# The ends of two routed mixture-of-experts stages in another order, with eight modulation products moved to a later stage

## The chip, the cores and the metric

One core of one Trainium2 chip runs the whole program. The metric is the device time of one execution in microseconds (us). The core's engines are TensorE (PE in the profile; PEld is its weight load), VectorE (DVE), ScalarE (ACT), GpSimd (POOL) and SyncE (SP), which issues the transfers.

## The reference

The program computes two blocks over 256 tokens of 1024 numbers in float32. The first has two layers. Each mixes tokens (attention of two kinds), normalizes, and then runs a routed mixture of 16 experts, two per token:

```python
def first_block(x, ...):
    for l in range(DEPTH):            # 2
        mix = even_mixer(...) if l % 2 == 0 else odd_mixer(...)
        x = layer_norm(ALPHA * x + mix, ln_g[l, 0], ln_b[l, 0])
        ffn = routed_moe(x, router_w, router_b, moe_w_gate[l], moe_w_up[l], moe_w_down[l])
        x = layer_norm(ALPHA * x + ffn, ln_g[l, 1], ln_b[l, 1])
    return x

# in routed_moe, for each expert e:
    h = jax.nn.silu(xt @ w_gate[e]) * (xt @ w_up[e])
    y = y + gates[:, e:e + 1] * (h @ w_down[e])
```

The second block has six sublayers (four swiglu feed-forwards, one hybrid recurrence, one mLSTM). In each, the input is normalized by its root mean square and shifted and scaled by a modulation vector, the product of a condition vector with a large matrix ("ada").

## The kernel before

There are ten stages, A to J, run in this order. A is the even attention (0 to about 131 us in the profile), B the routed experts of layer 0 (to about 361), C the odd attention (to about 475), D the routed experts of layer 1 (to about 709), E, G, H and J the feed-forwards, F the hybrid, I the mLSTM.

**Weights.** Nearly all time goes to matrix products with weights that are used once. SyncE streams them as transfers of 1 MB, two chunks of 128x1024 float32 each, into a ring of blocks (`load_weights`, L521); a transfer needs a free block, and a block is free when both of its chunks are used up. Most products are made of two halves of the weight: ScalarE copies a chunk to the shorter type fp32r (L598) and VectorE makes the difference to the original, again in fp32r (L599). TensorE multiplies with both (`mm`, L607). The expert stages use the chunks as they are and split the features instead. `SPLIT_AHEAD` gives the splits of a stage a priority by which the scheduler places them ahead of their use.

**Ada.** The modulation vectors don't use TensorE: VectorE multiplies a chunk with the broadcast condition vector and sums over the row (`ada_step`, L560). `ADA` says how many of the 144 chunks each stage takes, as running ends (A the first 15, C the next 10, E the next 35). A plan spreads them evenly over the stage's own chunks.

**Routed stages.** The 16 experts go in pairs 0 to 7. For each pair, `gate_up` makes two PSUM banks on TensorE; `hidden` runs silu on ScalarE (L1377) and a product on VectorE (L1378); `turn` transposes the result on TensorE (L612) and copies it out (L1386); `down` multiplies with the second weights and takes each half of the result out of PSUM twice, the high part by ScalarE (L1406) and the low part by VectorE (L1407); `combine` multiplies both with the gates and adds the result to x (L1426). Each pair's `turn`, `combine` and `down` run behind the next pair's `gate_up`. Behind `gate_up` of pair 5 all engines load a count and branch on it (`overflow`, L1441 and L1442): the branch's body deals with experts that got too many tokens, and isn't entered in these runs.

**The end of a routed stage.** For pairs 6 and 7, `combine` adds into four PSUM banks, one for each token half (t) and column half (n), which start with the product of the identity and x. `first_splits` makes the first splits of the next stage's weights here (three in B, four in D), and the evacuations of pair 7 are placed behind these (`first`). Then `normed` takes statistics of each bank (L816), their mean and variance (L821), the root (L822) and the affine part (L833 to L838), first for token half 0, then 1. The next stage starts on each token half: in C with transposes (L612), a copy (L1613) and a difference (L1614); in E with sums of squares (L874), a reciprocal root (L876 to L880), a scaling (L916), transposes and features (L683 to L691).

**Order.** Within `behind(...)` an instruction is placed after the named ones; `pinned()` places what is in it behind the last TensorE instruction. `spin` is a row of transposes of a constant whose result isn't used (`SPIN` has their counts: entry 3 stands between D and E, entry 4 between B and C).

Of the kernel before, what the change touches and what calls it, by code (L numbers as in the profile page):

```python
# [9 lines left out]
F32 = mybir.dt.float32  # L10
# [4 lines left out]
OP = mybir.AluOpType  # L15
# [40 lines left out]
ADA = {'A': 15, 'C': 25, 'E': 60, 'F': 64, 'G': 96, 'H': 132, 'I': 140, 'J': 144}  # L56
# [342 lines left out]
SPIN = 20, 12, 8, 50, 20  # L399
# [8 lines left out]
class Net:  # L408
    NBLK = 23

    def __init__(self, ctx, tc, aps, phases, plan=None, at=None):
        self.tc, self.nc, self.aps, self.phases = tc, tc.nc, aps, phases
        self.blk = ctx.enter_context(tc.tile_pool(name="blk", bufs=1))
        self.cst = ctx.enter_context(tc.tile_pool(name="cst", bufs=1))
        self.sm = ctx.enter_context(tc.tile_pool(name="sm", bufs=2))
        self.pp = ctx.enter_context(tc.tile_pool(name="pp", bufs=4, space=bass.MemoryType.PSUM))
        self.issue_at, self.at = plan, at or {}
        self.free = [(-64, 0, b) for b in range(self.NBLK if plan is not None else 64)]
        self.own, self.nfree = {}, 0
# [9 lines left out]
        self.pre, self.guard, self.guarded, self.ada_held, self.evac = [], [], 0, 0, None  # L429
        self.first, self.last, self.left = {}, {}, {}  # L430
# [368 lines left out]
    def normed(self, x, get, tok, gb=None):  # L799
# [9 lines left out]
        def fin(t, n, o):  # L809
# [5 lines left out]
            with self.behind(*first[:n]):  # L815
                v.bn_stats(st[:, t, n, :], o)  # L816
# [49 lines left out]
    def rstd(self, t):  # L866
# [8 lines left out]
        if n_ == 2:  # L875
            nc.vector.tensor_tensor(r, ss[:, 0:1], ss[:, 1:2], op=OP.add)  # L876
        else:
            nc.vector.tensor_reduce(r, ss[:, :n_], axis=AX.X, op=OP.add)
# [370 lines left out]
    def phase_moe(self, l):  # L1249
# [131 lines left out]
        def turn(h, hT):  # L1381
# [4 lines left out]
            nc.scalar.activation(hT, pt, AF.Copy)  # L1386
            return hT

        def down(pr, hT, gsl, nextw, then, first=()):
# [13 lines left out]
            def leave(n):  # L1403
                ns = PIECES[0][n]
                with self.behind(*first):
                    self.evac = nc.scalar.activation(yy[:, 0, ns], y[n], AF.Copy, scale=gsl[:, pr % 2, :])  # L1406
                    v.scalar_tensor_tensor(yy[:, 1, ns], y[n], gsl[:, pr % 2, :], yy[:, 0, ns].bitcast(F32),  # L1407
                                           op0=OP.mult, op1=OP.subtract)
                then(n, yy)

            for n in range(2):
                some(((n, 0), (n, 1)))
                some(((n, 2), (n, 3)))
                leave(n)
            return uy, yy

        def combine(pr, yy, PT, n, c=None):

            ns = PIECES[0][n]
            for t in range(2):  # L1420
                o = c[t, n] if c else self.ph()
                for j in range(2):
                    self.mm(o, PT[pr % 2][:, t * 128:(t + 1) * 128], yy[:, j, ns], j == 0 and not c,
# [109 lines left out]
        for s in range(8):  # L1533
# [36 lines left out]
        with pinned():  # L1570
            h = hs.pop(7)
            hT = turn(h, self.w2([128, 4, 128]))
            c = {}
            for t in range(2):
# [847 lines left out]
```

## Time and profile before

| | us |
|---|---|
| median of 3 runs (lowest to highest) | 1877.28 (1875.49 to 1878.21) |
| the profiled execution's own time | 1873.63 |
| its span | 1871.7 |
| TensorE busy | 1824.0 (97%) |
| VectorE busy | 1229.0 (66%) |
| ScalarE busy | 929.4 (50%) |
| mean of the transfers | 271 GB/s |

The share of an engine is a mean over stages with different limits. In a timeline row the first number is the time from the span's start, the second the duration of the group, "x8" the number of instructions in it, and the bracket the idle time of that engine before it and what ended it. TensorE's products of float32 (identity, `down`) appear as two records each, so that eight records are four products of the program; those of fp32r (`combine`) appear as one. PEclk is the granted clock as a share of full speed.

### The profile page before, as it was taken

What the parts mean: (1) busy time and instruction counts of PE and PEld (TensorE: products, weight loads), DVE (VectorE), ACT (ScalarE), POOL (GpSimd) and SP (SyncE); (2) the same over time, 40 slices, a digit from 0 to 9 for tenths busy, and PEclk for the clock granted to TensorE, in tenths of its full rate; (3) what the DMA queues carried; (4) which work ended last, traced back from release to release, by engine and by line L of the source; (5) the groups of instructions that cost most, each with busy time, mean ns of one, the idle gap of its engine ahead of it and who ended that gap; (6) DMA issues with size and microseconds to landing.
All of it is one profiled execution on the core that took longest, in us unless ns stands there. A gap on an engine that the chain in (4) does not pass through costs nothing.

```text
span 1871.7 us, 26716 instructions
## 1 busy us (share of the span) xinstructions
PE 1824.0 (97%) x10276; PEld 1398.1 (75%) x10276; DVE 1229.0 (66%) x2227; ACT 929.4 (50%) x1683; POOL 170.2 (9%) x176
## 2 busy tenths in 40 slices
PE   7999999999999999999999999999999999999998
PEld 7874544487545537888899788888888888888887
DVE  5961211497322228996689979876998676677673
ACT  5641111375221125556697655565556576666553
POOL 0000000020000000000152210001500101320001
PEclk9999999999999999999999999999999999999999
DMA  9869999665899996874436388837694625565520
GB/s 386 333 244 398 421 420 421 261 260 216 359 421 421 420 422 255 358 285 159 178 108 234 115 317 329 332 130 296 242 412 180 247 91 181 202 247 207 199 89 34
DMA packets 70967, 506.87 MB, mean 271 GB/s; under 512 B 7856, under 2 KB 8112, under 8 KB 10032
## 3 DMA queue, kind: packets, MB, share of 16 engines
q1 hardware_dynamic: 70256, 503.15, 67.7%
q8 instruction: 83, 1.36, 0.3%
q10 hardware_dynamic: 576, 1.93, 0.3%
q14 instruction: 52, 0.43, 0.1%
HBM read 504.00 MB, written 1.05 MB: 270 GB/s over the span
## 4 chain that ended last, share of the span: by engine, by line
PE 56%; DVE 4%; ACT 3%; POOL 1%; issue 1%; DMA 1%; DVEq 0%; ACTq 0%; POOLq 0%
PE ph L607 31%; PE pg L607 23%; PE ph L612 1%; DMA t<-in_weights 1%; DVE t L599 1%; ACT t L598 1%; ACT ph L874 1%; POOL t L1940 0%; DVE w L962 0%; DVE t L916 0%; DVE t L964 0%; POOL w L2293 0%; POOL w L1934 0%; ACT t L1884 0%; ACT rms L879 0%
## 5 line engine op out<-in xcount | busy, mean ns | idle before, releaser
L607 PE MATMUL pg<-t,t 128*128 128x512 f32 (+4 forms) x4702 | 932.4, 400 | 17.3 <-ACT t L598 8.2
L607 PEld LDWEIGHTS pg<-t,t 128*128 128x128 f32 (+1 forms) x4702 | 666.8, 178 | 229.0 <-issue 128.6
L607 PE MATMUL ph<-t,t 128*128 128x512 f32 (+3 forms) x3270 | 574.3, 335 | 3.2 <-ACT t L1718 1.2
L599 DVE TENSOR_TENSOR t<-t,t 128x1024 fp32r<-128x1024 f32 (+4 forms) x414 | 506.5, 1240 | 87.4 <-ACT t L598 85.8
L607 PEld LDWEIGHTS ph<-t,t 128*128 128x128 f32 (+1 forms) x3270 | 486.3, 188 | 73.3 <-ACT t L2304 1.9
L598 ACT ACTIVATE t<-t 128x1024 fp32r<-128x1024 f32 (+4 forms) x414 | 426.4, 1050 | 136.2 <-DVE t L599 45.6
L560 DVE SCALAR_TENSOR_TENSOR t<-t,cact 128x1024 f32<-128x1024 f32 x144 | 175.7, 1228 | 5.6 <-DMA t<-in_weights 5.6
L607 PE MATMUL ph<-t,w 128*64 128x512 f32 (+3 forms) x696 | 168.7, 559 | 0.0
L632 ACT ACTIVATE w<-ph 128x256 f32<-128x256 f32 x160 | 60.3, 378 | 157.1 <-PE ph L607 153.0
L607 PEld LDWEIGHTS ph<-t,w 128*64 128x64 f32 (+1 forms) x696 | 70.0, 148 | 77.9 <-issue 67.4
L1378 DVE TENSOR_TENSOR w<-w,pg 128x512 f32<-128x512 f32 x16 | 11.0, 685 | 167.6 <-ACT w L1377 167.6
L1377 ACT ACTIVATE w<-pg 128x512 f32<-128x512 f32 x16 | 9.6, 597 | 197.9 <-PE pg L607 197.9
L633 DVE TENSOR_TENSOR w<-w,ph 128x256 f32<-128x256 f32 x160 | 66.1, 416 | 46.1 <-ACT w L632 45.3
L1407 DVE SCALAR_TENSOR_TENSOR t<-ph,rgsl,t 128x512 fp32r<-128x512 f32 x32 | 24.0, 750 | 95.3 <-ACT t L1406 95.3
L1406 ACT ACTIVATE t<-ph,rgsl 128x512 fp32r<-128x512 f32 x32 | 21.9, 685 | 117.2 <-PE ph L607 113.8
L964 POOL TENSOR_TENSOR t<-t,w 128x512 f32<-128x512 f32 x12 | 15.7, 1306 | 645.0 <-DVE w L962 642.4
L667 ACT ACTIVATE t<-w 128x256 fp32r<-128x256 f32 x107 | 44.0, 412 | 52.7 <-DVE w L1860 43.9
L691 POOL TENSOR_TENSOR t<-w,t 128x256 fp32r<-128x256 f32 x30 | 30.1, 1018 | 372.2 <-DVE t L687 370.2
L607 PE MATMUL ph<-w,t 128*128 128x256 f32 (+2 forms) x384 | 51.9, 311 | 0.2 <-DVE t L1325 0.2
L607 PEld LDWEIGHTS ph<-w,t 128*128 128x128 f32 (+1 forms) x384 | 41.5, 178 | 13.2 <-issue 8.1
L668 DVE TENSOR_TENSOR t<-w,t 128x256 fp32r<-128x256 f32 x96 | 44.0, 459 | 9.3 <-ACT t L667 9.3
L874 ACT ACTIVATE ph<-t 128x512 f32<-128x512 f32 x28 | 16.8, 602 | 66.0 <-POOL t L964 39.9
(338 smaller groups left out, 1407.0 us busy)
## 6 DMA issues: line engine op xcount, KB each, us to landing
t<-in_weights SPq DMA_DIRECT2D x475, 1024.0 KB, 8.5
t<-in_xT SPq DMA_DIRECT2D x2, 512.0 KB, 5.4
t<-in_weights SPq DMA_DIRECT2D x2, 512.0 KB, 6.4
t<-in_x SPq DMA_DIRECT2D x1, 1024.0 KB, 13.6
t<-in_gate_cols ACTq DMA_DIRECT2D x1, 864.0 KB, 9.0
t<-in_consts_attn SPq DMA_DIRECT2D x1, 512.0 KB, 18.6
t<-in_final_g ACTq DMA_DIRECT2D x1, 512.0 KB, 3.5
out<-t SPq DMA_DIRECT2D x2, 256.0 KB, 2.0
```

What stands on the lines that cost most here:

```text
L560: self.nc.vector.scalar_tensor_tensor(w, w, 1.0, self.cact, op0=OP.mult, op1=OP.mult, accum_out=acc)
L598: a = self.nc.scalar.activation(t[:, 0, :n], w[:, :n], AF.Copy)
L599: b = self.nc.vector.tensor_tensor(t[:, 1, :n], w[:, :n], t[:, 0, :n].bitcast(F32), op=OP.subtract)
L607: self.last_mm = [self.nc.tensor.matmul(out, lhsT=a, rhs=b, start=start, stop=stop)]
L632: self.nc.scalar.activation(a, o[:, S:], AF.Copy)
L633: self.nc.vector.tensor_tensor(a, a, o[:, :S], op=OP.add)
L667: self.nc.scalar.activation(hi, src, AF.Copy)
L668: (eng or self.nc.vector).tensor_tensor(lo, src, hi.bitcast(F32), op=OP.subtract)
L691: i = e.tensor_tensor(f.part(1, k, 2)[:, :, ts], tmp, hh.bitcast(F32), op=OP.subtract)
L874: nc.scalar.activation(junk[:, :ns.stop - ns.start], xs, AF.Square, accum_out=ss[:, n:n + 1])
L1406: self.evac = nc.scalar.activation(yy[:, 0, ns], y[n], AF.Copy, scale=gsl[:, pr % 2, :])
L1407: v.scalar_tensor_tensor(yy[:, 1, ns], y[n], gsl[:, pr % 2, :], yy[:, 0, ns].bitcast(F32), op0=OP.mult, op1=OP.subtract)
```

## The change

1. `ADA`: A takes 7 chunks instead of 15, C still 10, E 43 instead of 35. Eight chunks, their transfers and VectorE's products with them, move from A to E.
2. `SPIN`: 30 instead of 50 transposes between D and E, none instead of 20 between B and C.
3. In `normed` both statistics of the second token half are placed behind the last affine instruction of the first, and the second of them behind the sum in `rstd` as well, where the next stage starts with that.
4. The silu and product of pair 5 are placed past the branch, behind the copy of `turn`.
5. At the end of a routed stage, combine 6 starts the banks; the first splits of the next stage stand behind pair 6's evacuations; the identity products come singly, each ahead of pair 7's combine into its bank; pair 7's combine of token half 0, n = 0, stands in the middle of the second half of `down`, and all of token half 1 at the very end.

```diff
-ADA = {'A': 15, 'C': 25, 'E': 60, 'F': 64, 'G': 96, 'H': 132, 'I': 140, 'J': 144}
+ADA = {'A': 7, 'C': 17, 'E': 60, 'F': 64, 'G': 96, 'H': 132, 'I': 140, 'J': 144}
...
-SPIN = 20, 12, 8, 50, 20
+SPIN = 20, 12, 8, 30, 0
...
@@ normed, fin(t, n, ...)
-            with self.behind(*first[:n]):
+            with self.behind(*first[:1], *[self.summed] * (n == 1 < len(first))):
                 v.bn_stats(st[:, t, n, :], o)
...
@@ rstd
-            nc.vector.tensor_tensor(r, ss[:, 0:1], ss[:, 1:2], op=OP.add)
+            self.summed = nc.vector.tensor_tensor(r, ss[:, 0:1], ss[:, 1:2], op=OP.add)
...
@@ turn, down, combine
-            nc.scalar.activation(hT, pt, AF.Copy)
+            self.turned = nc.scalar.activation(hT, pt, AF.Copy)
...
                 with self.behind(*first):
                     self.evac = nc.scalar.activation(yy[:, 0, ns], y[n], AF.Copy, scale=gsl[:, pr % 2, :])
-                    v.scalar_tensor_tensor(yy[:, 1, ns], y[n], gsl[:, pr % 2, :], yy[:, 0, ns].bitcast(F32),
-                                           op0=OP.mult, op1=OP.subtract)
-                then(n, yy)
+                    self.low = v.scalar_tensor_tensor(yy[:, 1, ns], y[n], gsl[:, pr % 2, :],
+                                                      yy[:, 0, ns].bitcast(F32), op0=OP.mult, op1=OP.subtract)
             for n in range(2):
                 some(((n, 0), (n, 1)))
-                some(((n, 2), (n, 3)))
+                if n and last:
+                    with pinned():
+                        then(0, yy)
+                    with pinned():
+                        some(((n, 2), (n, 3)))
+                else:
+                    some(((n, 2), (n, 3)))
                 leave(n)
+                if n or not last:
+                    then(n, yy)
...
-                    self.mm(o, PT[pr % 2][:, t * 128:(t + 1) * 128], yy[:, j, ns], j == 0 and not c,
+                    self.mm(o, PT[pr % 2][:, t * 128:(t + 1) * 128], yy[:, j, ns], j == 0 and (pr == 6 or not c),
                             j == 1 and (pr == 7 or not c))
...
@@ the loop over pairs
             if s == 5:
                 overflow(xg)
                 self.last_pe = None
-            hs[s] = hidden(*pgu)
+            else:
+                hs[s] = hidden(*pgu)
...
                     hT = turn(hs.pop(s - 1), self.w2([128, 4, 128]))
+                    if s == 5:
+                        with self.behind(self.turned):
+                            hs[s] = hidden(*pgu)
...
@@ the end
             hT = turn(h, self.w2([128, 4, 128]))
-            c = {}
-            for t in range(2):
-                for n, ns in enumerate(PIECES[t]):
-                    c[t, n] = self.pg()
-                    self.mm(c[t, n], self.ident, x[:, t, ns], True, False)
+            c = {(t, n): self.pg() for t in range(2) for n in range(2)}
             uy, yy = ys.pop(6)
-            for n in range(2):
-                combine(6, yy, PT[3], n, c)
+            low6 = self.low
+            combine(6, yy, PT[3], 0, c)
+        with pinned():
+            combine(6, yy, PT[3], 1, c)
             self.release(uy)
         last = [stream() for _ in range(8)]
-        self.first_splits()
+        with self.behind(self.evac, low6):
+            self.first_splits()
+
+        def own(t, n):
+            ns = PIECES[t][n]
+            with pinned():
+                self.mm(c[t, n], self.ident, x[:, t, ns], False, False)
+
+        def meet(n, yy):
+
+            own(0, n)
+            with pinned():
+                combine(7, yy, PT[3], n, c, (0,))
+            if n:
+                for m in range(2):
+                    own(1, m)
+                    with pinned():
+                        combine(7, yy, PT[3], m, c, (1,))
+
         with pinned():
-            uy, _ = down(7, hT, gsl[:, 6:], iter(last).__next__, lambda n, yy: combine(7, yy, PT[3], n, c),
-                         self.halved if self.pre else ())
+            uy, _ = down(7, hT, gsl[:, 6:], iter(last).__next__, meet, self.halved if self.pre else (), True)
```

Line numbers below L816 are one higher in the changed kernel (L599 for L598, L608 for L607), those in the routed stages one or two higher.

The first place is ScalarE's order at the end of stage B. t_2767 holds the result of pair 6, t_2822 that of pair 7, and t_2701 and t_2707 are the first weights of C. Before:

```order
L1406 ACTIVATE t_2767<-ph_2768,rgsl_1528 128x512
L598 ACTIVATE t_2813<-t_2701 128x968
L598 ACTIVATE t_2816<-t_2701 128x968
L1406 ACTIVATE t_2767<-ph_2769,rgsl_1528 128x512
L1386 ACTIVATE w_530_2790<-ph_2791 128x512
L598 ACTIVATE t_2819<-t_2707 128x968
L1406 ACTIVATE t_2822<-ph_2823,rgsl_1528 128x512
L1406 ACTIVATE t_2822<-ph_2824,rgsl_1528 128x512
```

Changed (t_2751 is pair 6, t_2802 pair 7, t_2685 and t_2691 the weights):

```order
L1408 ACTIVATE t_2751<-ph_2752,rgsl_1512 128x512
L1408 ACTIVATE t_2751<-ph_2753,rgsl_1512 128x512
L1387 ACTIVATE w_526_2774<-ph_2775 128x512
L599 ACTIVATE t_2793<-t_2685 128x968
L599 ACTIVATE t_2796<-t_2685 128x968
L599 ACTIVATE t_2799<-t_2691 128x968
L1408 ACTIVATE t_2802<-ph_2803,rgsl_1512 128x512
L1408 ACTIVATE t_2802<-ph_2804,rgsl_1512 128x512
```

Both evacuations of pair 6 and the copy of pair 7's transposes now stand ahead of the three copies of the splits.

The second place is TensorE's order there. The four banks are pg, kc is the identity and t_67 is x; ph_2823 and ph_2824 are the two halves of pair 7's `down`. Before:

```order
L612 MATMUL ph_2791<-kc,w_518_2737 128x128 x4
L607 MATMUL pg_2797<-t_67,kc 128x512
L607 MATMUL pg_2799<-t_67,kc 128x512
L607 MATMUL pg_2801<-t_67,kc 128x512
L607 MATMUL pg_2803<-t_67,kc 128x512
L607 MATMUL pg_2797<-t_2767,w_463_2491 128x512 x2
L607 MATMUL pg_2801<-t_2767,w_463_2491 128x512 x2
L607 MATMUL pg_2799<-t_2767,w_463_2491 128x512 x2
L607 MATMUL pg_2803<-t_2767,w_463_2491 128x512 x2
L607 MATMUL ph_2823<-t_2673,w_530_2790 64x512 x4
L607 MATMUL ph_2823<-t_2679,w_530_2790 64x512 x4
L607 MATMUL ph_2824<-t_2689,w_530_2790 64x512
```

Changed (the halves are ph_2803 and ph_2804):

```order
L613 MATMUL ph_2775<-kc,w_514_2721 128x128 x4
L608 MATMUL pg_2781<-t_2751,w_459_2475 128x512 x2
L608 MATMUL pg_2783<-t_2751,w_459_2475 128x512 x2
L608 MATMUL pg_2782<-t_2751,w_459_2475 128x512 x2
L608 MATMUL pg_2784<-t_2751,w_459_2475 128x512 x2
L608 MATMUL ph_2803<-t_2657,w_526_2774 64x512 x4
L608 MATMUL ph_2803<-t_2663,w_526_2774 64x512 x4
L608 MATMUL ph_2804<-t_2673,w_526_2774 64x512 x4
L608 MATMUL pg_2781<-t_67,kc 128x512
L608 MATMUL pg_2781<-t_2802,w_462_2485 128x512 x2
L608 MATMUL ph_2804<-t_2679,w_526_2774 64x512 x4
L608 MATMUL pg_2782<-t_67,kc 128x512
```

The identity products have left the head of the row; one stands ahead of each combine of pair 7, and the products of token half 1 (the banks pg_2783 and pg_2784) stand last.

The third place is VectorE's order in the middle of stage A, where t_84 to t_113 are blocks of the ring. Before:

```order
L599 TENSOR_TENSOR t_286<-t_84,t_286 128x1024
L560 SCALAR_TENSOR_TENSOR t_84,mod<-t_84,cact 128x1024
L560 SCALAR_TENSOR_TENSOR t_87,mod<-t_87,cact 128x1024
L599 TENSOR_TENSOR t_318<-t_87,t_318 128x1024
L560 SCALAR_TENSOR_TENSOR t_89,mod<-t_89,cact 128x1024
L599 TENSOR_TENSOR t_351<-t_89,t_351 128x1024
L1153 COPY t_278<-pg_324 64x256
L1003 CAST t_131<-w_49_383 8x256
L1004 TENSOR_TENSOR w_50_384<-w_49_383,t_131 8x256
```

Changed:

```order
L600 TENSOR_TENSOR t_285<-t_84,t_285 128x1024
L561 SCALAR_TENSOR_TENSOR t_84,mod<-t_84,cact 128x1024
L600 TENSOR_TENSOR t_317<-t_87,t_317 128x1024
L600 TENSOR_TENSOR t_347<-t_87,t_347 128x1024
L561 SCALAR_TENSOR_TENSOR t_89,mod<-t_89,cact 128x1024
L600 TENSOR_TENSOR t_397<-t_89,t_397 128x1024
L1154 COPY t_277<-pg_320 64x256
L1004 CAST t_131<-w_48_379 8x256
L1005 TENSOR_TENSOR w_49_380<-w_48_379,t_131 8x256
```

Of the three ada products (L560) in these rows two are left (L561), and a fourth split, of the second chunk of t_89, stands ahead of the copy of L1153 (now L1154); before, the fourth split took its chunk from t_113 and stood five rows behind these.

## Rows read from the trace of the kernel before

**Rows 1.** Page, busy us of each engine (share of the span), instructions

```profile
PE 1824.0 (97%) x10276; PEld 1398.1 (75%) x10276; DVE 1229.0 (66%) x2227; ACT 929.4 (50%) x1683; POOL 170.2 (9%) x176
```

**Rows 2.** Waits of TensorE: us in total, times, longest us

```profile
PE pg L607 <- ACT t L598: 8.2, 2, 7.6
PE pg L607 <- DVE t L599: 5.6, 5, 2.9
...
PE ph L612 <- DVEq L1442: 3.9, 2, 2.1
```

**Rows 3.** Timeline in stage A: start, us, instruction, [idle before <-releaser]

```profile
36.78 1.20 DVE L560 SCALAR_TENSOR_TENSOR t<-t,cact 128x1024 f32<-128x1024 f32 x1
...
37.02 0.50 PE L607 MATMUL pg<-t,t 128*128 128x256 f32 x2 [0.60 <-ACT t L598]
...
39.39 1.36 PE L607 MATMUL pg<-t,t 128*128 128x256 f32 x6 [1.87 <-DVE t L599]
```

**Rows 4.** Windows: us, busy (x) of each engine, PEclk, DMA share, GB/s

```profile
39.80:43.20 3.40, 3.40 (x16) 2.94 (x16) 2.42 (x6) 0.94 (x1) 0.00 (x0) 0.50 1.01 417
275.30:278.70 3.40, 3.40 (x18) 3.40 (x18) 1.09 (x2) 1.45 (x3) 0.00 (x0) 0.50 1.01 412
347.00:350.30 3.30, 3.30 (x10) 0.91 (x8) 0.00 (x0) 0.00 (x0) 0.00 (x0) 0.50 1.01 422
...
691.80:698.50 6.70, 5.47 (x13) 2.14 (x15) 2.31 (x3) 0.82 (x1) 0.00 (x0) 0.50 1.03 428
```

**Rows 5.** Timeline at the overflow branch, of B and of D

```profile
273.95 0.63 PE L612 MATMUL ph<-kc,w 128*128 128x128 f32 x4 [2.09 <-DVEq L1442]
...
620.77 0.63 PE L612 MATMUL ph<-kc,w 128*128 128x128 f32 x4 [1.81 <-DVEq L1442]
```

**Rows 6.** Windows, at the end of stage B

```profile
335.00:345.00 10.00, 9.02 (x35) 3.99 (x32) 2.82 (x3) 3.80 (x6) 0.00 (x0) 1.00 1.01 419
```

**Rows 7.** Timeline at the end of stage B

```profile
338.99 3.60 PE L607 MATMUL pg<-t,kc 128*128 128x512 f32 x8
...
341.89 1.91 ACT L598 ACTIVATE t<-t 128x968 fp32r<-128x968 f32 x2 [5.98 <-DMA t<-in_weights]
...
345.09 0.75 DVE L1407 SCALAR_TENSOR_TENSOR t<-ph,rgsl,t 128x512 fp32r<-128x512 f32 x1
...
345.89 0.97 PE L607 MATMUL pg<-t,w 128*128 128x512 f32 x3 [0.96 <-DVE t L1407]
...
355.27 3.65 PE L607 MATMUL ph<-t,w 128*64 128x512 f32 x12
...
358.96 0.69 ACT L1406 ACTIVATE t<-ph,rgsl 128x512 fp32r<-128x512 f32 x1 [6.07 <-PE ph L607]
...
361.06 2.34 PE L612 MATMUL ph<-kc 128*128 128x128 f32 x20
...
364.19 1.38 PE L612 MATMUL ph<-kc,t 128*128 128x128 f32 x8 [0.79 <-DVE t L838]
364.72 0.69 DVE L816 BATCH_NORM_STATS2 lnst<-pg 128x6 f32<-128x512 f32 x1
```

**Rows 8.** Timeline at the end of stage D, by engine

```profile
687.07 1.06 ACT L598 ACTIVATE t<-t 128x1024 fp32r<-128x1024 f32 x1 [9.86 <-DMA t<-in_weights]
...
707.02 0.69 ACT L1406 ACTIVATE t<-ph,rgsl 128x512 fp32r<-128x512 f32 x1 [6.07 <-PE ph L607]
...
692.89 1.22 DVE L599 TENSOR_TENSOR t<-t,t 128x1024 fp32r<-128x1024 f32 x1
...
715.00 1.07 PE L612 MATMUL ph<-kc,t 128*128 128x128 f32 x8 [0.27 <-DVE t L916]
```

**Rows 9.** Windows, in stage E

```profile
732.00:841.00 109.00, 109.00 (x577) 92.96 (x576) 106.69 (x171) 59.10 (x96) 0.00 (x0) 1.00 0.81 323
841.00:866.00 25.00, 25.00 (x133) 21.33 (x132) 15.93 (x23) 14.91 (x23) 0.00 (x0) 1.00 0.48 191
```

**Rows 10.** Groups of VectorE's instructions in E, 732 to 866 us

```profile
L560 DVE SCALAR_TENSOR_TENSOR t<-t,cact 128x1024 f32<-128x1024 f32 x34 | 40.9, 1216 | 0.0
```

More of the change, by code (lines that the diff above doesn't have):

```diff
@@ L429, in __init__ @@
         self.pre, self.guard, self.guarded, self.ada_held, self.evac = [], [], 0, 0, None
+        self.summed = None
         self.first, self.last, self.left = {}, {}, {}
@@ L1385, in turn, with down @@
                 self.tr(pt[:, k, :], h[:, k * 128:(k + 1) * 128])
-            nc.scalar.activation(hT, pt, AF.Copy)
+            self.turned = nc.scalar.activation(hT, pt, AF.Copy)
             return hT
-        def down(pr, hT, gsl, nextw, then, first=()):
+        def down(pr, hT, gsl, nextw, then, first=(), last=False):
             uy, yy = self.alloc([128, 2, 1024], F32R)
@@ L1406, in leave, with combine @@
                     self.evac = nc.scalar.activation(yy[:, 0, ns], y[n], AF.Copy, scale=gsl[:, pr % 2, :])
-                    v.scalar_tensor_tensor(yy[:, 1, ns], y[n], gsl[:, pr % 2, :], yy[:, 0, ns].bitcast(F32),
-                                           op0=OP.mult, op1=OP.subtract)
-                then(n, yy)
+                    self.low = v.scalar_tensor_tensor(yy[:, 1, ns], y[n], gsl[:, pr % 2, :],
+                                                      yy[:, 0, ns].bitcast(F32), op0=OP.mult, op1=OP.subtract)
             for n in range(2):
                 some(((n, 0), (n, 1)))
-                some(((n, 2), (n, 3)))
+                if n and last:
[5 more added lines that the diff above has]
+                    some(((n, 2), (n, 3)))
                 leave(n)
+                if n or not last:
+                    then(n, yy)
             return uy, yy
-        def combine(pr, yy, PT, n, c=None):
+        def combine(pr, yy, PT, n, c=None, ts=(0, 1)):
             ns = PIECES[0][n]
-            for t in range(2):
+            for t in ts:
                 o = c[t, n] if c else self.ph()
                 for j in range(2):
-                    self.mm(o, PT[pr % 2][:, t * 128:(t + 1) * 128], yy[:, j, ns], j == 0 and not c,
+                    self.mm(o, PT[pr % 2][:, t * 128:(t + 1) * 128], yy[:, j, ns], j == 0 and (pr == 6 or not c),
                             j == 1 and (pr == 7 or not c))
@@ L1572, in phase_moe @@
             hT = turn(h, self.w2([128, 4, 128]))
-            c = {}
-            for t in range(2):
-                for n, ns in enumerate(PIECES[t]):
-                    c[t, n] = self.pg()
-                    self.mm(c[t, n], self.ident, x[:, t, ns], True, False)
+            c = {(t, n): self.pg() for t in range(2) for n in range(2)}
             uy, yy = ys.pop(6)
-            for n in range(2):
-                combine(6, yy, PT[3], n, c)
+            low6 = self.low
+            combine(6, yy, PT[3], 0, c)
+        with pinned():
+            combine(6, yy, PT[3], 1, c)
             self.release(uy)
         last = [stream() for _ in range(8)]
-        self.first_splits()
+        with self.behind(self.evac, low6):
[13 more added lines that the diff above has]
+                        combine(7, yy, PT[3], m, c, (1,))
         with pinned():
-            uy, _ = down(7, hT, gsl[:, 6:], iter(last).__next__, lambda n, yy: combine(7, yy, PT[3], n, c),
-                         self.halved if self.pre else ())
+            uy, _ = down(7, hT, gsl[:, 6:], iter(last).__next__, meet, self.halved if self.pre else (), True)
         self.warm(AF.Sqrt, h)
```

## The prediction

> **What bounds the kernel now.** I read the page's busy times first. TensorE is busy 1824.0 us of the span of 1871.7 [rows 1], so all its idle time together is 47.7 us: a change that removes no TensorE work can win no more than a part of these, plus what the half-speed clock costs. Next, who TensorE waits for. The dearest releasers are the two halves of the weight split (ScalarE's fp32r copy and VectorE's difference) and VectorE's queue at the overflow branch [rows 2]. The timelines around these waits then give three places that the change touches: the middle of stage A, the branch of the routed stages B and D, and their ends. Last, the granted clock: each of four stretches reads 0.50, which is 1.2 of 2.4 GHz [rows 4]. A stretch of 3.4 us at half speed does 1.7 us of work, so it costs 1.7; the long one in D, 6.7 us, costs 3.35. They begin right behind idle time of TensorE: at 39.8 after waits of 0.60 and 1.87 [rows 3], at 275.3 after 2.09 [rows 5], at 347.0 after 0.96 [rows 7].
>
> The profiled execution took 1873.63 us, 3.65 less than the median of the three runs, 1877.28. I sum against the profiled one and carry the difference over to the median.
>
> **Stage A: −4.2.** At 36.78 VectorE runs an ada product of 1.20 us ahead of the split difference for which TensorE then waits; TensorE idles 0.60 and 1.87 us [rows 3], 2.47 together. With 7 instead of 15 chunks of ada, the order has no product there and the split comes next, out of an earlier transfer. The product is 1.20 us and the later split of ScalarE takes part, so the gain is between 1.2 and 2.47; I take all of it, since the split that TensorE waits for now has an earlier source as well. With the waits goes the stretch behind them [rows 4], 1.7: 4.2 in all. The lower end, 1.2 and no clock, is kept for the range. Eight half-MB transfers leave A's stream too. At 419 GB/s [rows 6] 1 MB takes 2.50 us, so that is 10 us of transfers. B's first weights wait for free blocks at A's end rather than for bandwidth, so I let B's whole stream move with A's end by 4.2 and by no more. If it moved by the 10 us, the ends below would gain up to 6 more; that is held for the lower end of the range.
>
> **The branch: nothing by itself.** The silu and product of pair 5 stand on ScalarE and VectorE ahead of the branch's load, so TensorE, which has only the transposes of pair 4 to do, waits 2.09 in B and 1.81 in D [rows 5]. Behind the change both engines reach the branch empty, and four products of TensorE move past it; about 0.3 is left. That would give 1.8 and the half-clock stretch in B (1.7), and 1.5 in D. I count none of it twice: weights stream at 419 GB/s with the transfers' share at 1.01 [rows 6], so what TensorE gains in mid-stage is given back where it waits for the last weights. It is needed for the next step, though.
>
> **End of B: −6.9.** Now the four identity products run first, 3.60 us, then combine 6 waits for its evacuation, which on ScalarE is queued behind two splits of C's first weights that could start only when these landed, at 341.89 [rows 7]. In the new order the evacuations of pair 6 come ahead of the splits. What is late next? The third split. Its transfer lands 2.50 behind the first, at about 344.4; ScalarE's copy takes 0.96 (half of 1.91), VectorE's difference about 1.22 [rows 8], so it ends at 346.6. Pair 7's first low evacuation is put behind it, 0.75 [rows 7]: 347.4. Then come a low product and eight records of the second half at 0.30 each (3.65 by 12), 2.4 with them: the last evacuation starts at about 349.8 instead of 358.96 [rows 7], 9.2 earlier. The check is TensorE's own work: from 338.99 to the evacuation at 358.96 are 19.97 us; less three identity products of the four (2.7), half a combine (0.7), the waits (1.9) and the clock (1.7) leave 13.0, so it could be there at 352.0. Less the 3.5 of the branch that is 348.5, before the splits are done. So the splits decide, by little, and TensorE waits some 1 to 3 us in front of them.
>
> From the last evacuation to the first transposes of C are 5.23 us now (358.96 to 364.19) [rows 7], and I keep that. The 20 spin transposes (2.34) go; behind the last first-token product stand now two identity products (1.8) and four gate products (0.97 by three, 1.3), 3.1 together, so the same gap is covered and costs nothing. If it weren't covered, it would be idle and not longer. Two statistics of the second token now stand between the first token's affine and VectorE's low half of C's features, where one stood, 0.69 [rows 7]: +0.6. Last, new waits are there for a clock to fall: +1.7. So −9.2 + 0.6 + 1.7 = −6.9.
>
> **End of D: −8.7.** The same build, with four splits out of two transfers. The first lands at 687.07 [rows 8], the second so at 689.6; two copies of 1.06 and the last difference of 1.22 end at about 693.0, the low evacuation at 693.8, product and second half at 696.2, against 707.02 [rows 8]: 10.8 earlier. From there to E's transposes stay 7.98 (715.00 less 707.02). One statistic of 0.7 moves into ScalarE's and VectorE's exchange on the first token; half of it shows, +0.4. A new half-clock stretch, +1.7. Sum −8.7. The spins, 30 instead of 50, are again replaced by the second token's products.
>
> **Stage E: +0.3.** Eight products of 1.216 us [rows 10], 9.7 of VectorE, move here. VectorE is busy 106.69 of 109.00 us in the first stretch and 15.93 of 25.00 in the next, while TensorE is at 100% in both [rows 9]. Idle are 2.3 and 9.1, 11.4 in all, so the eight fit, with 1.7 to spare, if the splits are far enough ahead to be late by up to 7.4 in the middle. That the engine at 98% keeps TensorE at 100% says that they are ahead; how far, these rows don't say. Bounds 0 and 9.7; I take 0.3, near the row that shows no wait.
>
> Sum: −4.2 − 6.9 − 8.7 + 0.3 = −19.5, 1854.1 for a profiled execution, 1857.8 for the median. Own range of this case 1853 to 1863: A at its lower end is +3, the branch's gain missing at the ends +2, the new clock stretches none or one longer.
>
> The row first: behind the wait of 1.81 us in D's branch [rows 5] no stretch at half speed follows in the trace, behind 2.09 in B one does [rows 4, 5]. The Trainium skill, "TensorE: Matmul & The Clock Gate", section "What's actually happening", says that "the default state is throttled, and activity releases the throttle". By that rule any longer wait that the new order leaves at the ends costs a stretch, as the sum has it; by D's row it may cost none, as in the first rival. The trace bears the rule out in the three places named above and leaves the size of the wait open.
>
> **Rivals.**
> 1. *The clock stays up at the new ends.* The waits that I expect are cut into pieces by products (identity and gate) that TensorE can do meanwhile. For: D's branch. Against: in B's end 0.96 behind a shorter wait was enough [rows 7]. Then −19.5 − 3.4 = −22.9: 1854.4. Chance 0.18.
> 2. *E's splits come late.* The eight products are not absorbed by the lead, and TensorE waits for VectorE's differences by up to 9.7: −19.8 + 9.7 = −10.1, 1867.2. For: 106.69 of 109 [rows 9]. Against: 9.1 idle right behind. 0.12.
> 3. *The ends keep their length.* Something else that lands or is freed late holds pair 7 as long as now, and only A (4.2) and the two half-clock stretches (1.7 and 3.35) go: −9.2, 1868.1. For: transfers are saturated. Against: ScalarE's queue order is what stood at 341.89 and 687.07. 0.10.
> 4. *Slower: VectorE becomes the bound in E.* From the point where the splits' lead is used up, each of the eight products is a wait of its own of 1.2, and, as at 39.8, each is followed by a half-clock stretch: 9.7 + 8 × 1.7 = 23.3. With −19.8 from the rest that is +3.5, 1880.8. For: the margin is 1.7 us over two stretches. Against: VectorE's idle 9.1 in the second, and TensorE without any wait. It decides if the lead is below the 7.4. 0.05.
> 5. *Nothing happens:* the waits are inferred, and the splits' landing holds A and both ends as now, whatever the order: 1877. 0.05.
>
> **How the numbers follow.** Forecast 0.50, rivals 0.18, 0.12, 0.10, 0.05 and 0.05. The time is the forecast's, 1857.8. The range starts at 1849 (B's stream earlier by up to 6 with a clock that stays up) and ends at 1868, which takes in rivals 1 and 2 and the nearer half of 3. A measurement of this kernel tells about 0.2% (3.8 us) from no change. Faster by over that: 0.50 + 0.18 + 0.12 + 0.10 = 0.90; within it 0.05; slower 0.05.
>
> **What would show it.** A: no ada product between 36 and 39 us, no wait of 1.87, no clock of 0.50 at 40. Branch: silu and product behind the branch and TensorE's wait for VectorE's queue under 0.5. Ends: both evacuations of pair 6 ahead of the splits on ScalarE, the last evacuation of pair 7 about 9 us (B) and 11 us (D) closer to the landing of the next stage's first weights, and between it and the transposes still 5 and 8 us. E: VectorE at 100% and TensorE without a wait for a split. The forecast is wrong if TensorE waits for VectorE in E, if the half-clock stretches at the ends grow instead of staying at one each, or if the next stage's first weights land later, counted from the stage's start, so that the splits hold pair 7 back.

## The result: 1854.86 us, and the profile after

The changed kernel took 1854.86 us, median of 4 runs (1852.18 to 1856.01); the kernel before 1876.38, median of 4 (1872.02 to 1878.21). The ratio is 0.9888, with a 95% interval of 0.9876 to 0.9901: 21.5 us less, where 19.5 were forecast (1857.8, from a median before of 1877.28). The profiled execution took 1852.18.

The page of the changed kernel, busy us of each engine as in [rows 1], and below it its waits of TensorE, to set beside [rows 2]:

```profile
PE 1809.9 (98%) x10236; PEld 1391.0 (75%) x10236; DVE 1229.2 (66%) x2227; ACT 929.9 (50%) x1683; POOL 172.2 (9%) x176
```

```profile
PE pg L608 <- ACT t L599: 7.5, 1, 7.5
...
PE pg L608 <- DVE t L600: 3.4, 3, 2.9
PE pg L608 <- DVE t L1409: 2.1, 3, 1.0
PE pg L608 <- ACT t L1408: 1.6, 2, 1.2
```

TensorE's idle time (span less busy) went from 47.7 to 40.3 us. TensorE's wait for VectorE's queue at the branch (then L1442) has left the list; 0.6 us in two waits for TensorE's own queue is left there. The 7.5 us on ScalarE's split are the first weights of the program, which wait in both kernels.

The table gives the start of the first transposes of TensorE (L612, now L613) at eight places. The first number is the time before, the others the difference to it in the profile of each kernel (the experiments are below).

| | before | change | 1 ada | 2 silu | 3 order | 4 ends | 5 ident. | 6 two | 7 E 59 | stat. | 8 again |
|---|---|---|---|---|---|---|---|---|---|---|---|
| B start | 128.01 | −4.60 | −4.88 | −1.98 | +0.49 | −0.10 | −4.25 | −4.51 | −4.20 | −4.27 | −4.55 |
| B, pair 7 | 338.50 | −7.55 | −7.81 | −5.00 | −1.02 | −1.60 | −4.19 | −7.45 | −4.09 | −7.21 | −7.47 |
| C, first | 364.19 | −12.82 | −14.59 | −1.52 | −5.12 | −10.37 | −10.02 | −16.07 | −10.62 | −13.19 | −12.87 |
| D start | 474.69 | −12.03 | −15.03 | −1.09 | −4.71 | −9.68 | −8.56 | −14.66 | −10.78 | −13.69 | −11.44 |
| D, pair 7 | 683.83 | −13.26 | −13.63 | −2.34 | −4.72 | −9.71 | −9.80 | −14.52 | −12.01 | −11.90 | −11.28 |
| E, first | 715.00 | −22.90 | −14.46 | −1.63 | −11.55 | −20.27 | −18.41 | −26.18 | −21.63 | −20.65 | −20.74 |
| behind E | 911.25 | −22.95 | −14.58 | −1.69 | −11.61 | −20.27 | −18.42 | −26.26 | −15.16 | −20.55 | −20.80 |
| in J | 1703.92 | −21.54 | −14.85 | −0.01 | −10.24 | −20.70 | −17.12 | −25.20 | −13.64 | −18.22 | −20.78 |

The change won 4.60 in A, 8.22 in B and 10.87 in D, lost 0.79 in C and 1.5 in F, and neither won nor lost in E (0.05 less). In F the clock fell after a wait of the same length as before.

**Stage A**, to set beside [rows 3] (time, duration, instruction); first an ada product of the kernel before, then the changed kernel:

```profile
26.67 1.22 DVE L560 SCALAR_TENSOR_TENSOR t<-t,cact 128x1024 f32<-128x1024 f32 x1
```

```profile
26.85 2.36 DVE L600 TENSOR_TENSOR t<-t,t 128x1024 fp32r<-128x1024 f32 x2 [0.21 <-ACT t L599]
...
35.25 2.40 PE L608 MATMUL pg<-t,t 128*128 128x256 f32 x18
...
37.31 1.22 DVE L600 TENSOR_TENSOR t<-t,t 128x1024 fp32r<-128x1024 f32 x1
...
38.12 0.96 PE L608 MATMUL pg<-t,t 128*128 128x256 f32 x6
```

Where the ada product stood at 26.67, VectorE now makes two differences in a row, so that between 24 and 32 us it makes four instead of three. TensorE works on products with split weights from 35.25 to 37.65, where it had waited. The next difference starts at 37.31, the TensorE row behind it has no idle time, and the clock doesn't fall there. A new wait of 0.68 comes at 44.81.

**The branch**, B and D, beside [rows 5]; TensorE now waits 0.30 for its own queue:

```profile
265.85 0.63 PE L613 MATMUL ph<-kc,w 128*128 128x128 f32 x4 [0.30 <-PEq L1451]
...
607.23 0.63 PE L613 MATMUL ph<-kc,w 128*128 128x128 f32 x4 [0.30 <-PEq L1451]
```

**End of B**, beside [rows 7]:

```profile
331.06 0.69 ACT L1408 ACTIVATE t<-ph,rgsl 128x512 fp32r<-128x512 f32 x1 [2.75 <-PE ph L608]
...
336.37 1.91 ACT L599 ACTIVATE t<-t 128x968 fp32r<-128x968 f32 x2 [4.06 <-DMA t<-in_weights]
...
339.51 1.01 ACT L599 ACTIVATE t<-t 128x968 fp32r<-128x968 f32 x1 [1.23 <-DMA t<-in_weights]
...
340.43 0.67 ACT L1408 ACTIVATE t<-ph,rgsl 128x512 fp32r<-128x512 f32 x1
...
341.15 0.51 PE L608 MATMUL pg<-t,w 128*128 128x512 f32 x1 [1.19 <-ACT t L1408]
341.64 0.74 DVE L1409 SCALAR_TENSOR_TENSOR t<-ph,rgsl,t 128x512 fp32r<-128x512 f32 x1
...
342.44 0.50 PE L608 MATMUL pg<-t,w 128*128 128x512 f32 x1 [0.78 <-DVE t L1409]
...
342.87 3.15 PE L608 MATMUL ph<-t,w 128*64 128x512 f32 x8
...
346.06 0.69 ACT L1408 ACTIVATE t<-ph,rgsl 128x512 fp32r<-128x512 f32 x1 [4.96 <-PE ph L608]
...
351.37 1.23 PE L613 MATMUL ph<-kc,t 128*128 128x128 f32 x8 [0.65 <-DVE t L839]
```

ScalarE takes both parts of pair 6 out before the splits (here its second evacuation, at 331.06). Then the third split waits for its transfer until 339.51, pair 7's first evacuation for that split, and TensorE 1.19 and 0.78 us for the two parts. The 8 records behind run at half speed. The last evacuation starts at 346.06, the transposes 5.31 later (5.23 before).

**End of D**, by engine, beside [rows 8]:

```profile
674.84 2.00 ACT L599 ACTIVATE t<-t 128x1024 fp32r<-128x1024 f32 x2 [2.92 <-DMA t<-in_weights]
677.38 2.00 ACT L599 ACTIVATE t<-t 128x1024 fp32r<-128x1024 f32 x2 [0.54 <-issue]
679.29 0.67 ACT L1408 ACTIVATE t<-ph,rgsl 128x512 fp32r<-128x512 f32 x1
683.97 0.69 ACT L1408 ACTIVATE t<-ph,rgsl 128x512 fp32r<-128x512 f32 x1 [4.02 <-PE ph L608]
...
680.75 0.74 DVE L1409 SCALAR_TENSOR_TENSOR t<-ph,rgsl,t 128x512 fp32r<-128x512 f32 x1
...
680.01 0.50 PE L608 MATMUL pg<-t,w 128*128 128x512 f32 x1 [0.44 <-ACT t L1408]
681.54 0.49 PE L608 MATMUL pg<-t,w 128*128 128x512 f32 x1 [1.03 <-DVE t L1409]
...
692.09 1.06 PE L613 MATMUL ph<-kc,t 128*128 128x128 f32 x8 [0.18 <-DVE t L917]
```

The same chain with four splits: the first landing at 674.84, the second at 677.38, low part at 680.75, last evacuation at 683.97, transposes 8.12 later (7.98 before). The wait here is 0.44 and 1.03 long, and no stretch at half speed follows.

**Windows**, granted clock last but two, beside [rows 4] and [rows 9]:

```profile
343.50:346.80 3.30, 3.30 (x9) 0.76 (x4) 0.20 (x2) 0.69 (x1) 0.00 (x0) 0.50 1.02 425
381.10:384.40 3.30, 2.87 (x11) 2.60 (x11) 3.12 (x10) 0.76 (x3) 1.24 (x1) 0.50 0.02 5
944.30:947.60 3.30, 3.30 (x18) 3.30 (x16) 3.30 (x4) 2.12 (x3) 0.00 (x0) 0.50 0.66 278
```

```profile
709.10:818.10 109.00, 109.00 (x577) 93.15 (x576) 107.90 (x171) 59.28 (x97) 0.00 (x0) 1.00 0.89 356
818.10:843.10 25.00, 25.00 (x133) 21.30 (x133) 23.04 (x39) 14.15 (x23) 0.00 (x0) 1.00 0.55 211
```

Half-clock stretches, apart from the run's last microseconds: five before [rows 4], among them 6.8 us in D and one of 3.4 in C at 394.8; three of 3.4 after (B's end, C, F). That is 20.4 us at half speed against 10.2, so 5.1 of the 21.5 us are clock. In E VectorE now works 107.90 and 23.04 us, 8.3 more than in [rows 9], and TensorE still stays at 100%.

### The profile page after: what moved, and what is told of

It is laid out like the page before. It is cut to its first block, busy times and chain, and to the rows that moved or that the text cites. A ratio compares the mean times of both kernels' runs of the same rounds, so it can differ in the third digit from the quotient of the medians.

```text
span 1850.2 us, 26644 instructions
## 1 busy us (share of the span) xinstructions
PE 1809.9 (98%) x10236; PEld 1391.0 (75%) x10236; DVE 1229.2 (66%) x2227; ACT 929.9 (50%) x1683; POOL 172.2 (9%) x176
## 4 chain that ended last, share of the span: by engine, by line
PE 57%; DVE 4%; ACT 3%; POOL 1%; issue 1%; DMA 1%; DVEq 0%; POOLq 0%; ACTq 0%
PE ph L608 31%; PE pg L608 24%; PE ph L613 1%; DVE t L600 1%; DMA t<-in_weights 1%; ACT t L599 1%; ACT ph L875 1%; POOL t L1968 0%; DVE w L963 0%; DVE t L917 0%; DVE t L965 0%; POOL w L2321 0%; POOL w L1962 0%; ACT t L1912 0%; POOL t L1964 0%
## 5 line engine op out<-in xcount | busy, mean ns | idle before, releaser
L608 PE MATMUL pg<-t,t 128*128 128x512 f32 (+4 forms) x4702 | 931.3, 400 | 15.1 <-ACT t L599 7.5
L608 PEld LDWEIGHTS pg<-t,t 128*128 128x128 f32 (+1 forms) x4702 | 666.6, 179 | 225.6 <-issue 128.5
L608 PE MATMUL ph<-t,t 128*128 128x512 f32 (+3 forms) x3270 | 574.3, 335 | 3.1 <-ACT t L1746 1.2
L608 PEld LDWEIGHTS ph<-t,t 128*128 128x128 f32 (+1 forms) x3270 | 486.3, 188 | 73.1 <-issue 1.8
L599 ACT ACTIVATE t<-t 128x1024 fp32r<-128x1024 f32 (+4 forms) x414 | 426.6, 1050 | 130.1 <-DVE t L600 44.4
L561 DVE SCALAR_TENSOR_TENSOR t<-t,cact 128x1024 f32<-128x1024 f32 x144 | 176.4, 1231 | 4.8 <-DMA t<-in_weights 4.8
L608 PE MATMUL ph<-t,w 128*64 128x512 f32 (+3 forms) x696 | 162.6, 551 | 0.0
L608 PEld LDWEIGHTS ph<-t,w 128*64 128x64 f32 (+1 forms) x696 | 68.8, 145 | 72.7 <-issue 62.5
L608 PE MATMUL ph<-w,t 128*128 128x256 f32 (+2 forms) x384 | 50.9, 306 | 0.2 <-DVE t L1326 0.2
L608 PEld LDWEIGHTS ph<-w,t 128*128 128x128 f32 (+1 forms) x384 | 40.1, 172 | 14.1 <-issue 8.5
```

Source lines behind the costliest of these rows:

```text
L561: self.nc.vector.scalar_tensor_tensor(w, w, 1.0, self.cact, op0=OP.mult, op1=OP.mult, accum_out=acc)
L599: a = self.nc.scalar.activation(t[:, 0, :n], w[:, :n], AF.Copy)
L608: self.last_mm = [self.nc.tensor.matmul(out, lhsT=a, rhs=b, start=start, stop=stop)]
```

## The experiments

Ratios are against the kernel before, run on the same chip, with a 95% interval; the times are medians of 4 to 12 runs unless one run is said.

**1. The ada chunks alone.**

```diff
-ADA = {'A': 15, 'C': 25, 'E': 60, ...
+ADA = {'A': 7, 'C': 17, 'E': 60, ...
```

> The kernel before with the move of the eight ada chunks alone (A 7, C 10, E 43). Theory (the product ahead of the split is what TensorE waited for in A; the whole stream moves with A's end; E's VectorE has room): 4.6 us at the end of A, as the changed kernel's trace has it, kept through B, C and D, and 0 to 0.3 lost in E, so -4.3 to -4.6 in all, ratio about 0.9976. Rival 1 (the gain of A is given back where the last weights of B land): 0 at C's first transposes and in all. Rival 2 (E's splits come late): up to +9.7 in E, +5 in all, ratio 1.003.

Measured: 1859.51 us, ratio 0.9919 (0.9906 to 0.9933), 15.6 us less instead of 4.6. A gave 4.88 and E lost nothing (the table), as the theory had it, and rival 2 falls. But B gave another 9.7: the scheduler put B's branch and end in the new order although their code is the old one. The timeline of B's end in this kernel:

```profile
330.80 0.69 ACT L1406 ACTIVATE t<-ph,rgsl 128x512 fp32r<-128x512 f32 x1 [2.75 <-PE ph L607]
...
336.99 1.91 ACT L598 ACTIVATE t<-t 128x968 fp32r<-128x968 f32 x2 [4.94 <-DMA t<-in_weights]
...
339.43 1.02 ACT L598 ACTIVATE t<-t 128x968 fp32r<-128x968 f32 x1 [0.53 <-DMA t<-in_weights]
...
343.74 0.69 ACT L1406 ACTIVATE t<-ph,rgsl 128x512 fp32r<-128x512 f32 x1 [2.73 <-PE ph L607]
...
349.60 1.38 PE L612 MATMUL ph<-kc,t 128*128 128x128 f32 x8 [1.19 <-DVE t L838]
```

The evacuation of pair 6 stands ahead of the splits, and although the identity products still come first, TensorE has no wait up to the last evacuation at 343.74. C's transposes come 1.5 us earlier than in the whole change, counted from B's start. D kept its old order, and its end gave 0.8 (−13.63 to −14.46). C's mark can't speak on rival 1, since B's end has a new order; D's can: with the old order there, a start 15.03 earlier gave an end 14.46 earlier, so what is won ahead of an old end is kept but for 0.6, and rival 1 falls too. So this run shows A and E; the parts of the change aren't independent in B.

**2. Silu and product of pair 5 past the branch, alone.** The diff is that of the change (the loop over pairs).

> The kernel before with silu and product of pair 5 past the branch alone. Theory (the landing of the next stage's first weights holds the ends, so what the branch gives is given back there): pair 7's transposes 2.9 us earlier in B and 1.2 in D, the next stage's transposes 0 to 0.5 earlier, in all -0.5 to +1 us, ratio 0.9997 to 1.0005. Rival (TensorE's own work holds the ends): the gain stays, -4 in all, ratio 0.9978.

Measured: 1875.21 us, ratio 1.0001 (0.9992 to 1.0010). In the table pair 7's transposes come 3.0 earlier in B, counted from B's start, and C's first 0.5 later than before, counted the same way (in D 1.25 and 0.54 earlier). The waits of B show where it went, first the one of the kernel before, then those of this run:

```profile
344.43 0.50 PE L607 MATMUL pg<-t,w 128*128 128x512 f32 x1 [0.91 <-ACT t L1406]
```

```profile
340.03 1.91 ACT L598 ACTIVATE t<-t 128x968 fp32r<-128x968 f32 x2 [9.12 <-DMA t<-in_weights]
...
342.56 0.80 PE L607 MATMUL pg<-t,w 128*128 128x512 f32 x1 [4.04 <-ACT t L1406]
...
344.03 1.65 PE L607 MATMUL pg<-t,w 128*128 128x512 f32 x3 [0.67 <-DVE t L1407]
```

0.91 before has become 4.04, with the splits landing at the same time after B's start, and the clock falls for 6.8 us. The theory holds: what the branch gives is given back in front of the landing.

**3. Only the order of splits and evacuations.** The kernel before, with one step of the change (`self.low` is the instruction of L1407, named):

```diff
             uy, yy = ys.pop(6)
+            evac6, low6 = self.evac, self.low
...
-        self.first_splits()
+        with self.behind(evac6, low6):
+            self.first_splits()
```

> The kernel before with one line of the change: the first splits of the next stage behind pair 6's two evacuations; identity products first, spins, branch and ada as before. Theory (ScalarE's queue is what TensorE waited for): the waits of 0.91 and 0.96 in B and of 0.84, 0.84, 0.18 and 1.30 in D go, and with them the half-clock stretches of 1.7 and 3.4: -3.6 in B, -6.5 in D, -10 in all, ratio 0.9946. Rival (the place of the identity products is what counts): under -3, ratio 0.9985 or more.

Measured: 1863.48 us, ratio 0.9935 (0.9921 to 0.9949), 12 us. The ends gave 4.1 in B (−1.02 to −5.12) and 6.8 in D (−4.72 to −11.55). Of the whole change's 5.27 and 9.64 at these places, the one line gives most. The theory holds.

**4. The new ends without the ada move and without the branch.**

> The changed kernel with the ada chunks and the silu of pair 5 where they were: the new ends, statistics and spins alone. Theory (the landing of the next stage's weights holds the new ends, so the branch adds nothing to them): -8 to -9.9 in B (the latter if no half-clock stretch follows), -9 to -10.9 in D, +0.8 in C, in all -17 to -20, ratio 0.990. Rival (the parts add up, TensorE's own work holds the ends): -21.5 less 4.6, 2.9 and 1.2, so -12.8, ratio 0.9932.

Measured: 1853.52 us, ratio 0.9884 (0.9869 to 0.9899): as much as the whole change. B gave 10.27 and D 10.59 counted from their starts, C's loss is 0.69. B's end has only a wait of 0.28 left, so no half-clock stretch; nor did the clock fall at the branch. B is a little beyond the theory's range and D in it, and the rival (12.8) falls: with the new ends the branch adds nothing in B. The 4.6 of A are missing, and yet the time is no longer than that of the whole change. In the profiles B makes up 2.05 of them and F 1.5, for the most part by stretches at half speed that this execution didn't have. The runs say the same: the granted clock of the four is 0.997 in the mean, that of the changed kernel's four 0.995, which is about 3.7 us over the span. So next to the new ends the ada move and the branch aren't shown to shorten the program; why the clock falls more often in the changed kernel wasn't tried.

**5. Identity products first again**, the rest as changed.

```diff
+            for t in range(2):
+                for n, ns in enumerate(PIECES[t]):
+                    self.mm(c[t, n], self.ident, x[:, t, ns], True, False)
...
         def own(t, n):
+            return
```

> The changed kernel with the four identity products back at the head of the end, as before; the rest as changed. Theory (the landing of the splits holds pair 7's first evacuation, so TensorE has 1.97 us of waits in B's end and 1.75 in D's to fill): in B no wait and so no half-clock stretch, C's transposes 1 to 1.7 us earlier than in the changed kernel; in D 0 to 1.2 later; in all -21 to -23 against the kernel before, ratio 0.988 to 0.989. Rival (the later place of the identity products is a gain of its own): 2.7 us lost at each end, -16, ratio 0.9915.

Measured: 1854.26 us, ratio 0.9882 (0.9867 to 0.9897), as the change itself. B's end gave 5.83 against 5.27, D's 8.61 against 9.64. The wait in front of B's last evacuation is 0.37 in all, and no stretch at half speed stands there; but the gain is 0.6 where 1 to 1.7 were expected, and counted from B's start C's transposes come 2.4 later, since in this execution the clock fell for 6.8 us behind B's start and pair 7 came 3.0 later. The rival falls. The place of the identity products is no gain of its own: in B they fill the wait in front of the splits, in D they are 1.0 too long for it.

**6. Two splits ahead of pair 7's first evacuation, the rest behind it.** This came from the 1.19 and 0.78 us above.

```diff
-            self.first_splits()
+            self.first_splits(2)
...
                 leave(n)
+                if last and not n:
+                    with self.behind(self.evac, self.low):
+                        self.other_splits()
```

> The changed kernel, but pair 7's first evacuation stands behind two of the next stage's splits, and the third (in D the third and fourth) behind that evacuation. Theory (the third split holds pair 7): the low evacuation comes when the products are done, 2.1 us earlier in B and 2.4 in D, and in B the half-clock stretch of 1.7 goes with the wait: -3.8 and -2.4, in all about -27.5 against the kernel before, ratio 0.9853. Rival (TensorE's own work or the last landing holds the ends): no change to the changed kernel, ratio 0.9885.

Measured: 1847.14 us, ratio 0.9850 (0.9837 to 0.9864): 28.3 us less than before, the fastest kernel of this study. B's end gave 8.62 (3.35 more than the change), D's 11.66 (2.0 more). The timeline of B's end:

```profile
336.37 1.91 ACT L599 ACTIVATE t<-t 128x968 fp32r<-128x968 f32 x2 [3.98 <-DMA t<-in_weights]
...
338.19 0.67 ACT L1415 ACTIVATE t<-ph,rgsl 128x512 fp32r<-128x512 f32 x1
...
340.06 1.01 ACT L599 ACTIVATE t<-t 128x968 fp32r<-128x968 f32 x1 [1.20 <-issue]
...
340.81 1.95 PE L608 MATMUL ph<-t,w 128*64 128x512 f32 x8
...
342.81 0.69 ACT L1415 ACTIVATE t<-ph,rgsl 128x512 fp32r<-128x512 f32 x1 [1.74 <-PE ph L608]
...
348.12 1.23 PE L613 MATMUL ph<-kc,t 128*128 128x128 f32 x8 [0.64 <-DVE t L839]
```

The evacuation goes out at 338.19, between the second and the third split, and TensorE has no wait longer than 0.11 up to the last evacuation at 342.81. So the third split did hold pair 7, as the prediction's chain has it.

The same kernel with the silu back in its place, one run:

> The kernel with two splits ahead of pair 7's first evacuation, with silu and product of pair 5 in their old place in the program; in B the scheduler puts them past the branch all the same, so that only D's branch has its wait of 1.8 us again. Theory (in this kernel TensorE's own work holds D's end, with no wait left there, so what the branch gives is kept): E's first transposes 1.2 to 1.5 us later, counted from D's start, than with the silu past the branch. Rival (the landing holds the end, as with the old ends): 0.

Measured: 1853.82 us in that run. Both executions had a half-clock stretch at D's start. From the last transposes ahead of D's branch (595.65 before) to E's first it gained 11.64 against 12.89: 1.25 less. The branch is worth its wait only where the end has no wait left.

**7. Sixteen more ada chunks in E**, taken from G.

```diff
-ADA = {... 'E': 60, 'F': 64, 'G': 96, ...
+ADA = {... 'E': 76, 'F': 80, 'G': 96, ...
```

> The changed kernel with sixteen more ada chunks in E (59 instead of 43) and as many fewer in G. Theory (E's VectorE had 11.4 us idle in its first 134 and 13 in the next 35; eight products took 8.3 of them, sixteen more of 1.3 each are 20.8 against some 15): the lead of the splits is used up, TensorE waits for VectorE's differences, 6 to 10 us in E, each longer wait with a half-clock stretch, in all -12 to -16 against the kernel before, ratio 0.9925. Rival (the lead is long enough for all): 0 in E, -21.5 in all, ratio 0.9885.

Measured: 1860.69 us, ratio 0.9921 (0.9907 to 0.9934). E lost 6.5 (−21.63 to −15.16). The windows of E and the end of it:

```profile
711.00:820.00 109.00, 109.00 (x577) 93.09 (x576) 108.35 (x172) 55.64 (x93) 0.00 (x0) 1.00 0.98 397
820.00:845.00 25.00, 25.00 (x133) 21.30 (x133) 24.02 (x41) 12.68 (x20) 0.00 (x0) 1.00 0.74 284
845.00:885.00 40.00, 39.45 (x207) 33.19 (x206) 37.21 (x65) 24.56 (x39) 1.29 (x1) 1.00 0.49 196
```

```profile
889.34 0.88 DVE L917 TENSOR_SCALAR t<-t,rms 128x512 f32<-128x512 f32 x2
...
889.97 1.27 PE L613 MATMUL ph<-kc,t 128*128 128x128 f32 x8 [4.36 <-DVE t L917]
```

VectorE is full: 108.35, 24.02 and 37.21 of 109, 25 and 40 us. The theory's sum holds, its place doesn't: inside E TensorE waited 0.55 us for one split and no more. The backlog came out once, at E's end, where the next stage's scaling (L917) stood behind it on VectorE, 4.36 us, with a half-clock stretch of 3.4 behind. It is not a wait per product.

**The statistics where they were**, one profile:

> The changed kernel with the second token half's first statistic where the order of before lets it go, ahead of the first half's affine. Theory: its 0.70 us stands in VectorE's chain from the last evacuation to the transposes, so these come 0.5 to 0.7 later in both ends, and in B the difference of C's features 0.7 earlier again; 0 to +1 in all. Rival (the statistic is hidden behind ScalarE's root): no change of either mark.

TensorE's wait for the affine was 1.23 us in B (0.65 in the change) and 0.64 in D for the scaling (0.18): 0.6 and 0.5, as the theory says. The wait for the difference of C's features (L1642) was 0.24 instead of 0.57: 0.33 back, where 0.7 was expected. The run took 1855.50 us.

**8. The changed kernel once more**, unaltered, one run.

> The changed kernel unaltered, profiled once more. In the first profile TensorE's clock fell at 343 (end of B), 381 (C) and 944 (F). Theory (what a wait of 0.8 to 2.9 us does to the clock differs from one execution to the next): the same waits at the same places within 0.1 us, but at least one stretch at half speed at another place, and the time differs by 1.7 us for each. Rival (the order of the instructions alone decides): the clock falls at the same three places.

Measured: 1852.96 us. The waits are the same: 1.19 and 0.78 at B's end, 1.24 at 383.06 in C, 2.88 in F. The clock fell at 343.8, as in the first profile, at 354.1 (behind C's first transposes) and at 466.7 (behind D's), but not behind the 1.24 in C and not in F. The wait of F in the first profile of the change (its window, 944.3 to 947.6, stands above), then in this one, with the window behind it:

```profile
943.49 2.79 PE L608 MATMUL pg<-t,t 128*128 128x256 f32 x14 [2.88 <-DVE t L600]
```

```profile
945.64 2.54 PE L608 MATMUL pg<-t,t 128*128 128x256 f32 x19 [2.88 <-DVE t L600]
```

```profile
945.70:949.00 3.30, 3.30 (x27) 3.14 (x28) 3.24 (x6) 3.29 (x4) 0.00 (x0) 1.00 0.74 303
```

The same instructions, the same 2.88 us, granted 0.50 in one execution and 1.00 in the other. The theory holds.

## Why the prediction was right

The profiled sum was −19.5, the profiles differ by 21.45. The median, 1854.86, lies nearer to rival 1's 1854.4 than to the forecast's 1857.8; the trace stands between the two: of the stretches at the new ends B's came and D's didn't. Part by part (the table):

- **A, −4.2: 4.60 measured**, 4.88 with the ada move alone. The size is right. Of the two reasons named, the missing product of 36.78 and the earlier transfer, the rows show the second: the product gone at 26.67 made room for a fourth difference, out of an earlier transfer, and TensorE worked on it where it had waited before. The difference that stood behind the product of 36.78 came 0.82 earlier, of which 0.65 is the earlier chain ahead of it. 1.7 of the gain is a clock that needn't fall: experiment 2 had the same waits of 0.60 and 1.87 there and no stretch.
- **The branch, nothing by itself:** right, and shown by experiment 2 and, for the other side, by the last part of 6.
- **End of B, −6.9: 8.22 measured.** The chain is as forecast. The last evacuation was put 221.8 us behind B's start (349.8 less 128.01), plus 1.7 for the new stretch; it came at 222.6 with the stretch, of which 1.2 fell ahead of it (3.15 us for the eight records instead of 1.95). What was mis-sized: eight records at full speed last 1.95 us (experiment 6), not 2.4, since the row of 12 records from which I took 0.30 each covers eight products, which would be 16 records; the first landing came 0.9 us earlier, counted from B's start, and the third split started 3.1 behind the first instead of 2.5. The +0.6 for the statistics doesn't belong to this mark: from the last evacuation to the transposes are 5.31 instead of 5.23, and the difference of C's features behind them is what comes later (C, below).
- **End of D, −8.7: 10.87 measured.** The last evacuation was put 221.5 us behind D's start, and came 221.3 behind. The term that failed is the new half-clock stretch, +1.7: the waits of 0.44 and 1.03 had none behind them, and in none of the eight profiles with the new ends did the clock fall there. That is rival 1, at one end of the two. That any longer wait costs a stretch was read into the sentence that the prediction quotes, which doesn't say it, and D's end shows that it isn't so. The statistic took 0.14 (8.12 less 7.98), not 0.4.
- **E, +0.3: nothing lost.** VectorE had the room. The margin is small, as experiment 7 shows, but rival 4's mechanism, a wait and a stretch for each product, is not what happens when it is used up.
- **The spins, nothing:** they weren't changed alone. From the last evacuation of B to C's transposes are 5.22 with the 20 of them (experiment 3) and 5.31 without. But the clock fell within 3 us of C's first transposes in 4 of the 8 profiles without them and in none of the 4 with them, which is too few to tell.
- **C: 0.79 lost**, where three waits on VectorE (at 353.7, 388.2 and 399.8) are longer by 0.3, 0.2 and 0.5. The first is for the difference of C's features, 0.57 instead of 0.24: this is what the prediction had counted as +0.6 to the end of B, and with the statistic put back it goes (the run behind experiment 7). The other two were not foreseen; experiments 2 and 3 lose 0.4 in C and have the last one too, and why was not tried.
- **Not foreseen either:** 1.5 in F, which is chance (experiment 8). The 2.3 of C and F hide that A, B, D and E together gave 4.2 more than forecast.
- **A step that holds only in part:** "the ends" were treated as the work of the new code. Experiment 1 shows that in B the scheduler makes the same order when only the ada chunks move. With the ada move given, the new code of B's end gave nothing there: C's transposes came 1.5 us later, about what the stretch at half speed behind its waits costs. Its gain is that of D.

## What to carry to other kernels

An evacuation queued behind a copy that waits for a transfer makes the matrix engine wait for that transfer; let only as many of the next stage's copies stand ahead of it as have landed by then (here two of three or four), which was worth 28 us together with the rest. Time won in mid-stage is worth nothing while a saturated stream of weights sets the stage's end, so mend the end first. Where a scheduler places the instructions, read its order for every part of an edit: a move in stage A changed the order 200 us later.

## What the runs showed of the hardware

Whether TensorE's clock falls behind a given wait isn't settled by the kernel. The wait of 2.9 us in F was followed by half speed in 8 of the 12 profiles of this study; the one of 0.77 at D's start in 5, the one of 0.77 at A's end in 3. Each fall costs 1.7 us for 3.4 us at 1.2 GHz, or twice that, so executions of one kernel differ by some us (the four of the changed kernel by 3.8, with granted clocks of 0.996 to 0.994), and a part of the size of 1.7 is to be read from the starts of instructions, not from the total. The Trainium skill, "TensorE: Matmul & The Clock Gate", section "What's actually happening", says that the gate watches activity in a rhythm of its own that doesn't start with the kernel and calls the number of slow products at a kernel's start "run-variable" for that reason. Experiment 8 fits that; no run here shows the rhythm itself.
